# 1/rms by token from the row form by 32x32 turns on VectorE, in place of two-column matmuls, in a fused decoder layer on one core

## The chip, the cores and the metric

One core of a Trainium2 chip runs the whole program. Its engines take their instructions in order, each from its own queue, and wait for each other by semaphores: TensorE (PE in the profile; PEld is its weight load), VectorE (DVE), ScalarE (ACT), GpSimd (POOL) and SyncE (SP), which here only issues DMAs. The metric is the device time of one execution in microseconds (us), as the median of several runs. A profile is one further execution, recorded by the hardware; its times count from the first instruction.

## The reference, cut to what matters

One decoder layer over 512 tokens of 1024 features, with a fixed memory of 256 tokens. What bears on the change are two of its norms and what is computed from them:

```python
def rms_norm(x, g):
    xf = x.astype(jnp.float32)
    var = jnp.mean(xf * xf, axis=-1, keepdims=True)
    return (xf * lax.rsqrt(var + EPS) * g.astype(jnp.float32)).astype(x.dtype)
...
        h = rms_norm(x, norm_mix[l])
        proj = h @ w_in[l]
        q_a, k_a, v_a, u_b, gate_b, gate_c, g_a, g_b = jnp.split(proj, split_points, axis=-1)
...
        x = x + memory_cross_attention(rms_norm(x, norm_mem_q[l]), rms_norm(mem, norm_mem_kv[l]),
                                       w_mem_q[l], w_mem_kv[l], w_mem_o[l])
```

Stick-breaking attention (8 heads of 64) on q, k, v, a gated short convolution, two gated branch projections and an output projection follow the first line; keys and values of the memory come from `rms_norm(mem, ...)`. A SwiGLU feed-forward part and a final norm end the layer.

## The kernel before

All matrices are split in two parts, high and low, and a product is three matmuls (high x high, high x low, low x high), made by `mm3` at lines 176 to 178. Weights come by DMA as 128x1024 tiles `wr`; ScalarE casts the high part `wh` (L167), VectorE subtracts for the low part `wl` (L170).

The norm's factor 1/rms is not applied to the activations but to the products, so it is needed in two forms. *Along* the free axis, the same on all 128 partitions, it scales outputs that have tokens along the row (q, k, gates, the convolution; `r0b` for the mixer, 512 wide, and `rmb` for the memory, 256 wide). *By token*, one number for each partition, it scales outputs that have tokens on the partitions: the attention's values `v` (through `r0`) and the memory's values `vm` (through `rm`). `squares_mean` (L198) holds both. Given the sums of squares `acc`, split in `acch` and `accl`, `along` multiplies them by a 128x128 matrix of 1/1024 into `varb` (two matmuls, L218); `by_token` uses each 128-token piece as the stationary side against two columns of that matrix, into `var` (L209): eight matmuls with 128x2 outputs for 512 tokens, four for 256. `rstd_of` (L124) then makes 1/sqrt by Ln and Exp on ScalarE and one Newton step on VectorE, once for each form.

Round the first use of these factors the program runs as follows. TensorE makes the value products `v` of all tokens (L282), then `varb` and `var`, then the projections `pr`, column block by column block. `stacked` (L262) evicts the values: ScalarE scales the high part by `r0` (L268), VectorE makes the low part (L269), eight times each. `qk_part` (L312) scales a `pr` by `r0b` into q or k and splits it; the later half of q is also copied by DMA into `late_q` (`lq` in the profile, L321), with zeros in the other head's rows, so that the two heads of a pair are scored by one matmul of 256 or 512 columns.

`scores` (L394) multiplies keys by queries into the bank `z` and makes from it, with e^-|z| and ln, log(1 + e^z) in `e` (L417 to L420), masked by GpSimd (L376). `parts` (L429) splits `e` in `l` (ScalarE L390, VectorE L391). `weights` (L449) adds `negtri` times `l` into the same bank `z` (L454), which gives the log of the attention weights; ScalarE takes exp (L462). The steps go over four head pairs and four key blocks; between them TensorE makes further `pr` blocks from the list `fill`. Within the loop over the steps TensorE's order is that of the code (`manual_schedule`); before that loop, and for ScalarE, VectorE, GpSimd and SP throughout this stage, the framework's scheduler sets the order from its own estimates and priorities. The first call, `scores(*steps[0])`, stands ahead of the loop, so where its three matmuls stand among the `pr` is the scheduler's choice.

The memory's sums of squares are gathered along the attention's steps; at step `MEAN_AT` = 14 `rm` and `rmb` are made. `mem_scale` is a part of the later memory sublayer; `mem_v` uses `rm`. `eps_sq` (L1129) belongs to the feed-forward part's norm, and `cu` (L340) is the convolution's input, in two buffers of 128x514.

Of the kernel before, what the change touches and what calls it, by code (L numbers as in the profile page):

```python
# [8 lines left out]
F32 = mybir.dt.float32  # L9
# [4 lines left out]
P = 128  # L14
D = 1024
S = 512
KD = D // P
TT = S // P
# [20 lines left out]
MEAN_AT = 14  # L39
# [11 lines left out]
def hybrid_layer(ctx: ExitStack, tc: tile.TileContext, xT_d, memT_d, cols_d, wv_d, win_d,  # L51
                 wbr_d, wmix_d, wmq_d, wmk_d, wmv_d, wmo_d, wfi_d, wfo_d, wfp_d, gain_d, wga_d, out):
    nc = tc.nc

    cpool = ctx.enter_context(tc.tile_pool(name="cpool", bufs=1))
# [13 lines left out]
    def nm(s):  # L69
        count[0] += 1  # L70
        return f"{s}{count[0]}"

    def unit(s, cols=512):
        return upool.tile([P, cols], F32R, tag="u", name=nm(s), padded_shape=[P, 512])

    def tmp(s, cols=512):
        return tpool.tile([P, cols], F32, tag="t", name=nm(s), padded_shape=[P, 512])

    def f(ap):
        return ap.bitcast(F32)  # L80
# [105 lines left out]
    def split(src, s, scale=None, cols=512, new=unit):  # L186

        hi, lo = new(s + "h", cols), new(s + "l", cols)
        if scale is None:
            casts.append(nc.scalar.copy(hi, src))  # L190
            los.append(nc.vector.tensor_tensor(out=lo, in0=src, in1=f(hi), op=ALU.subtract))
        else:
            nc.scalar.activation(hi, src, AF.Copy, scale=scale)
            nc.vector.scalar_tensor_tensor(out=lo, in0=src, scalar=scale, in1=f(hi),
                                           op0=ALU.mult, op1=ALU.subtract)
        return hi, lo

    def squares_mean(acc, n):  # L198

        parts = unit("acch", n * P), unit("accl", n * P)  # L200
        nc.vector.tensor_copy(parts[0], acc)
        nc.vector.tensor_tensor(out=parts[1], in0=acc, in1=f(parts[0]), op=ALU.subtract)

        def by_token(s, tables=(), bank=otile):

            vp = bank("var")
            for t in range(n):
                for i in range(2):
                    nc.tensor.matmul(vp[:, 2 * t:2 * t + 2], parts[i][:, t * P:(t + 1) * P],  # L209
                                     mean_r[:, 0:2], start=i == 0, stop=i == 1)  # L210
            return rstd_of(vp[:, 0:2 * n].rearrange("p (t two) -> p t two", two=2)[:, :, 0], n, s,
                           tables)

        def along(s, tables=(), bank=otile, keep=None):

            vp = bank("varb")[:, :n * P]
            for i in range(2):
                nc.tensor.matmul(vp, mean_r, parts[i], start=i == 0, stop=i == 1)  # L218
            return rstd_of(vp, n * P, s, tables, keep=keep)

        return by_token, along


    xg, wv = [], []
    acc0 = tmp("acc")
    x_raw = [f(unit("xk")) for _ in range(KD)]
# [33 lines left out]
    mean0 = squares_mean(acc0, TT)  # L260

    def stacked(src, scale, odd):  # L262


        u = unit("v").rearrange("p (a s d) -> p a s d", s=2, d=HD)
        hi, lo = u[:, :, odd, :], u[:, :, 1 - odd, :]
        src = src.rearrange("p (a b d) -> p a b d", b=2, d=HD)[:, :, odd, :]
        nc.scalar.activation(hi, src, AF.Copy, scale=scale)  # L268
        nc.vector.scalar_tensor_tensor(out=lo, in0=src, scalar=scale, in1=f(hi), op0=ALU.mult,  # L269
                                       op1=ALU.subtract)  # L270
        return u
# [3 lines left out]
    for k in range(KD):  # L275

        terms = ((0, 0), (0, 1), (1, 0))
        for some in ((term,) for term in terms) if k == 0 else (terms,):
            for t in range(TT):
                sl = slice(t * P, (t + 1) * P)  # L280
                for a, b in some:
                    nc.tensor.matmul(vps[t], xg[k][a][:, sl], wv[k][b],  # L282
                                     start=k == 0 and (a, b) == (0, 0),
                                     stop=k == KD - 1 and a == 1)
    r0b, r0 = mean0[1]("r0b"), mean0[0]("r0")
    v = [[stacked(vps[t], r0[:, t:t + 1], h) for h in range(2)] for t in range(TT)]


# [36 lines left out]
    def gate(m, j):  # L325
        ps = project((O_A, O_B)[j] + m * P)
        t = gates[m, j] = tmp("g")
        both.append(nc.vector.tensor_tensor(out=t, in0=ps, in1=r0b, op=ALU.mult))
# [172 lines left out]
    def mem_square(k2):  # L501

        mk = f(unit("mk")).rearrange("p (j t) -> p j t", j=2)
        load_mem(k2, mk)
        nc.scalar.activation(accm if k2 == 0 else mk, mk, AF.Square)
        if k2 > 0:
            nc.vector.tensor_tensor(out=accm, in0=accm, in1=mk, op=ALU.add)
        if k2 == KD // 2 - 1:
            nc.vector.tensor_tensor(out=accm[:, 0, :], in0=accm[:, 0, :], in1=accm[:, 1, :],
                                    op=ALU.add)  # L510
# [19 lines left out]
    def fill_some(to):  # L530
        while fill and n_fill - len(fill) < to:
            g, *args = fill.pop(0)
            g(*args)
# [5 lines left out]
    with tc.manual_schedule(engines={mybir.EngineType.PE}):  # L539
        for i in range(len(steps) + 1):  # L540
            if i in MEM_AT:
                mem_square(MEM_AT.index(i))
            if i == MEAN_AT - 2:
                mean = squares_mean(accm[:, 0, :], MT)
            fill_some(n_fill * sum(shares[:i + 1]) / sum(shares))
            if i == MEAN_AT:
                with tc.high_priority(150):
                    rm = mean[0]("rm", bank=mmtile)
            if i + 1 < len(steps):
                scores(*steps[i + 1])  # L550
            if i < len(steps):
                weights(*steps[i])
            else:
                gate(EARLY, 0)
            if i + 1 < len(steps):
                parts(*steps[i + 1])
            if i > 0:
                values(*steps[i - 1])
            if i == MEAN_AT:
                with tc.high_priority(150):  # L560
                    rmb = mean[1]("rmb", bank=mmtile)
# [433 lines left out]
    def mem_scale():  # L995
        r1 = mean1[0]("r1", log_exp_tables(casts[-1]))
        nc.vector.tensor_scalar(out=r1s, in0=r1, scalar1=(D // MH) ** -0.5, scalar2=None,
                                op0=ALU.mult)

    km, vm, mq, scs, prs, pts = [], [[None] * 2 for _ in range(MT)], {}, {}, {}, {}  # L1000

    def mem_k(m):
# [14 lines left out]
    def mem_v(n):  # L1017
        pss = [mmtile("vm") for _ in range(MT)]
        for c in range(4):
            w = load_w(wmv_d[n, c], 512)  # L1020
            for j in range(2):
                k = 2 * c + j
                for t in range(MT):
                    sl = slice(t * P, (t + 1) * P)
                    mm3(pss[t], (mg[k][0][:, sl], mg[k][1][:, sl]),
                        (w[0][:, j, :], w[1][:, j, :]), k == 0, k == KD - 1)
        for t in range(MT):
            vm[t][n] = split(pss[t], "vm", rm[:, t:t + 1])

    def mem_q(h):  # L1030
        b = banks.pop(QM + h)
# [94 lines left out]

    rms, eps_sq = f(unit("rms")), cpool.tile([P, S], F32, tag="eps_sq", name="eps_sq")  # L1129
    eps_t4 = spool.tile([P, TT], F32, tag="epst", name="epst", bufs=1)  # L1130
    eps_d = cpool.tile([P, P], F32, tag="eps_d", name="eps_d")
    yt = {}
# [26 lines left out]
    with tc.manual_schedule(engines={mybir.EngineType.PE, mybir.EngineType.Activation,  # L1159
# [6 lines left out]
        for n, (m, i) in enumerate(uses):  # L1166
# [25 lines left out]
            if (m, i) == (1, 6):  # L1192
# [3 lines left out]
                for t in range(TT):  # L1196
                    rows = slice(t * P // TT, (t + 1) * P // TT)
# [162 lines left out]
    with tc.manual_schedule(engines={mybir.EngineType.PE, mybir.EngineType.Activation,  # L1360
# [28 lines left out]
        r = norm(t)  # L1389
# [78 lines left out]
```

## Time and profile before

| what | value |
|---|---|
| median of 3 runs | 846.53 us (846.05 to 846.75) |
| the profiled execution, its span | 847.03 us, 845.3 us |
| granted TensorE clock, mean | 0.997 |
| moved by DMA | 120.47 MB |

The span reaches from the first to the last instruction; the profiled execution's own time has 1.7 us around it. A row of a timeline gives the start in us from the span's start, the duration in us, the engine, the line, the operation, what it writes and reads, the shapes, and a count where equal neighbours are merged; a bracket at its end tells how long the engine had been idle and what it waited for. A duration of a matmul includes its way through the array: matmuls of 512 columns follow each other at about 0.23 us though each is shown with 0.39.

### The profile page before, as it was taken

How to read it: one execution, taken by the hardware profiler on the slowest of the kernel's cores; microseconds unless marked ns; L12 is line 12 of the kernel's file. 1: busy time of each engine (PE TensorE's matmuls, PEld its weight loads, DVE VectorE, ACT ScalarE, POOL GpSimd, SP SyncE). 2: the span in 40 equal slices, each digit the busy share in tenths (PEclk: the TensorE clock that was granted, in tenths of full speed). 3: DMA queues.
4: the chain of work that ended last, by engine and by line, in shares of the span. 5: the costliest groups of instructions: out<-in, count | busy, mean ns of one | idle time of the engine just before them, and what ended most of it. 6: DMA issues, size and time to landing. Idle time of an engine off the chain costs nothing.

```text
span 845.3 us, 13478 instructions
## 1 busy us (share of the span) xinstructions
PE 835.7 (99%) x5095; PEld 748.2 (89%) x5095; DVE 669.3 (79%) x1152; ACT 482.9 (57%) x873; POOL 88.5 (10%) x113
## 2 busy tenths in 40 slices
PE   9999999999999999999999999999999999999996
PEld 7888787888899988999988899999999999888885
DVE  8769889987856867978775889888877778895764
ACT  7556767566534555766554766555455556554434
POOL 1011112210100011000000111211111110110013
PEclk9999999999999999999999999999999999999998
DMA  8332332314745484555331437777777763870112
GB/s 299 128 122 64 108 104 66 111 51 167 206 104 146 148 251 128 162 178 194 129 115 56 112 86 202 189 185 177 179 182 178 180 156 125 269 216 26 51 50 100
DMA packets 50257, 120.47 MB, mean 143 GB/s; under 512 B 5136, under 2 KB 8208, under 8 KB 50192
## 3 DMA queue, kind: packets, MB, share of 16 engines
q1 hardware_dynamic: 40656, 101.49, 36.2%
q0 software_dynamic: 9248, 17.83, 13.0%
q8 instruction: 40, 0.66, 0.3%
q10 hardware_dynamic: 288, 0.29, 0.1%
q14 instruction: 25, 0.20, 0.1%
HBM read 116.42 MB, written 2.10 MB: 140 GB/s over the span
## 4 chain that ended last, share of the span: by engine, by line
PE 99%; DVE 0%; ACT 0%; issue 0%; DVEq 0%; ACTq 0%
PE z L775 20%; PE y L775 10%; PE pr L176 6%; PE pr L177 6%; PE pr L178 6%; PE v L775 5%; PE r L176 3%; PE r L178 3%; PE r L177 3%; PE f L177 3%; PE f L176 3%; PE f L178 3%; PE v L282 3%; PE br L177 2%; PE br L176 2%; PE br L178 2%
## 5 line engine op out<-in xcount | busy, mean ns | idle before, releaser
L167 ACT CAST wh<-wr 128x1024 fp32r<-128x1024 f32 x82 | 85.6, 1048 | 51.8 <-PE pr L177 11.3
L170 DVE TENSOR_TENSOR wl<-wr,wh 128x1024 fp32r<-128x1024 f32 x82 | 99.9, 1222 | 18.7 <-ACT wh L167 17.9
L775 PE MATMUL z<-xdh,wf 128*128 128x256 f32 x480 | 94.6, 282 | 0.0
L176 PE MATMUL pr<-xgh,wh 128*128 128x512 f32 x224 | 87.8, 392 | 0.0
L178 PE MATMUL pr<-xgh,wl 128*128 128x512 f32 x224 | 87.3, 390 | 0.0
L177 PE MATMUL pr<-xgl,wh 128*128 128x512 f32 x224 | 87.3, 390 | 0.0
L775 PEld LDWEIGHTS z<-xdh,wf 128*128 128x128 f32 x480 | 77.5, 189 | 0.3 <-issue 0.2
L775 PE MATMUL z<-xdl,wf 128*128 128x256 f32 x240 | 67.0, 279 | 0.0
L799 ACT COPY sa<-z 128x256 f32<-128x256 f32 x52 | 19.4, 373 | 74.1 <-PE z L775 74.0
L766 DVE TENSOR_TENSOR wf<-s,wf 128x512 fp32r<-128x512 f32 x60 | 41.4, 691 | 22.8 <-ACT wf L765 21.6
L725 POOL DMA_DIRECT2D ws<-in_w_ffn_in_dram x22 | 26.5, 1203 | 299.0 <-DVE c L619 109.5
L752 DVE TENSOR_TENSOR wf<-wg,wf 128x1024 fp32r<-128x1024 f32 x30 | 36.8, 1226 | 18.1 <-ACT wf L749 18.1
L178 PEld LDWEIGHTS pr<-xgh,wl 128*128 128x128 f32 x224 | 42.0, 188 | 8.9
L176 PEld LDWEIGHTS pr<-xgh,wh 128*128 128x128 f32 x224 | 42.1, 188 | 8.6 <-DVE rv L135 0.3
L177 PEld LDWEIGHTS pr<-xgl,wh 128*128 128x128 f32 x224 | 42.1, 188 | 8.3
L775 PE MATMUL y<-xch,wf 128*128 128x256 f32 x240 | 49.0, 286 | 0.0
L775 PE MATMUL z<-xch,wf 128*128 128x256 f32 x240 | 48.1, 283 | 0.0
L775 PEld LDWEIGHTS z<-xdl,wf 128*128 128x128 f32 x240 | 45.4, 189 | 0.2
L177 PE MATMUL f<-wl,acth 128*128 128x512 f32 (+1 forms) x116 | 44.3, 382 | 0.0
L176 PE MATMUL f<-wh,acth 128*128 128x512 f32 (+1 forms) x116 | 44.3, 382 | 0.0
L178 PE MATMUL f<-wh,actl 128*128 128x512 f32 (+1 forms) x116 | 44.1, 382 | 0.0
L766 DVE TENSOR_TENSOR wf<-ws,wf 128x512 fp32r<-128x512 f32 x60 | 40.9, 682 | 1.4 <-ACT wf L765 1.3
(357 smaller groups left out, 2466.3 us busy)
## 6 DMA issues: line engine op xcount, KB each, us to landing
wr<-in_w_in_dram SPq DMA_DIRECT2D x28, 512.0 KB, 3.5
ws<-in_w_ffn_in_dram SPq DMA_DIRECT2D x22, 512.0 KB, 3.8
ws<-in_w_ffn_in_dram POOLq DMA_DIRECT2D x22, 512.0 KB, 5.8
wg<-in_w_ffn_in_dram SPq DMA_DIRECT2D x22, 512.0 KB, 4.2
wr<-in_w_ffn_out_dram SPq DMA_DIRECT2D x14, 512.0 KB, 4.4
a<-in_w_ffn_in_dram SPq DMA_DIRECT2D x22, 256.0 KB, 4.4
wr<-in_w_branch_dram SPq DMA_DIRECT2D x8, 512.0 KB, 3.5
wr<-in_w_mix_out_dram SPq DMA_DIRECT2D x8, 512.0 KB, 3.7
```

Source lines behind the costliest of these rows:

```text
L167: after(nc.scalar.copy(h2, raw), lead[-1:] + waiting[:1])
L170: lows.append(nc.vector.tensor_tensor(out=l2, in0=raw, in1=f(h2), op=ALU.subtract))
L176: nc.tensor.matmul(ps, a[0], b[0], start=start, stop=False, **kw)
L177: nc.tensor.matmul(ps, a[0], b[1], start=False, stop=False, **kw)
L178: nc.tensor.matmul(ps, a[1], b[0], start=False, stop=stop, **kw)
L282: nc.tensor.matmul(vps[t], xg[k][a][:, sl], wv[k][b], start=k == 0 and (a, b) == (0, 0), stop=k == KD - 1 and a == 1)
L725: nc.gpsimd.dma_start(s13, a[:, 0:4:3, :], accum_op=ALU.add)
L752: nc.vector.tensor_tensor(out=lo, in0=pair, in1=f(hi), op=ALU.subtract)
L766: nc.vector.tensor_tensor(out=lo, in0=raw, in1=f(hi), op=ALU.subtract)
L775: nc.tensor.matmul(ps[:, :HS], a, b, start=i < 3 and k == 0 and j == 0, stop=k == KP - 1 and j == 2, skip_group_check=True)
L799: nc.scalar.copy((s[:, :HS], None, None, s[:, HS:], t[:, :HS], t[:, :HS])[i], z)
```

## The change

`by_token_of` is new. It takes the row form, where all 128 partitions hold the same numbers, and for each of the four groups of 32 partitions turns one 32x32 block of each 128-token piece on VectorE: group g takes the tokens 32g to 32g + 31 of every piece. After the turn, partition 32g + i holds the factor of token 32g + i of piece t in each of 32 columns, and column 0 is used. This gives `r0` from `r0b` (four instructions on 32 partitions x 128 elements) and `rm` from `rmb` (four of 32 x 64). The calls of `by_token` for the mixer and the memory go, with their narrow matmuls, Ln, Exp and Newton step; the query norm of the memory sublayer (`r1`) keeps its own. `rm` is written in `mem_scale` now. `eps_sq` takes a buffer of `cu` instead of one of its own.

```diff
+    def by_token_of(row, s):
+
+        n = row.shape[1] // P
+        r = cpool.tile([P, n, 32], F32, tag=s, name=nm(s))
+        for g in range(TT):
+            rows = slice(32 * g, 32 * g + 32)
+            nc.vector.transpose(out=r[rows, :, :],
+                                in_=row.rearrange("p (t c) -> p t c", c=P)[rows, :, rows])
+        return r[:, :, 0]
...
-    r0b, r0 = mean0[1]("r0b"), mean0[0]("r0")
+    r0b = mean0[1]("r0b")
+    r0 = by_token_of(r0b, "r0")
...
-            if i == MEAN_AT:
-                with tc.high_priority(150):
-                    rm = mean[0]("rm", bank=mmtile)
...
+        rm.append(by_token_of(rmb, "rm"))
+
+    rm = []
...
-            vm[t][n] = split(pss[t], "vm", rm[:, t:t + 1])
+            vm[t][n] = split(pss[t], "vm", rm[0][:, t:t + 1])
...
-    rms, eps_sq = f(unit("rms")), cpool.tile([P, S], F32, tag="eps_sq", name="eps_sq")
+    rms, eps_sq = f(unit("rms")), cpool.tile([P, S], F32, tag="cu", name="eps_sq",
+                                                 bufs=2, padded_shape=[P, S + 2])
```

How the queues read after it, at three places (the changed file has other line numbers, and its buffers other numbers). TensorE at the end of the value products, before:

```order
L218 MATMUL varb_332<-accl_229,mean_r 128x512
L209 MATMUL var_345<-mean_r,acch_228 128x2
L209 MATMUL var_345<-mean_r,accl_229 128x2
L209 MATMUL var_345<-mean_r,acch_228 128x2
L209 MATMUL var_345<-mean_r,accl_229 128x2
L209 MATMUL var_345<-mean_r,acch_228 128x2
L209 MATMUL var_345<-mean_r,accl_229 128x2
L209 MATMUL var_345<-mean_r,acch_228 128x2
L209 MATMUL var_345<-mean_r,accl_229 128x2
L176 MATMUL pr_407<-xgh_152,wh_403 128x512
```

and TensorE there after the change:

```order
L218 MATMUL varb_332<-acch_228,mean_r 128x512
L218 MATMUL varb_332<-accl_229,mean_r 128x512
L176 MATMUL pr_393<-xgh_152,wh_389 128x512
L177 MATMUL pr_393<-xgl_153,wh_389 128x512
L178 MATMUL pr_393<-xgh_152,wl_390 128x512
L176 MATMUL pr_393<-xgh_157,wh_389 128x512
```

The eight matmuls into `var` are gone, and `pr` follows `varb`.

TensorE at the first scores. Before, the last two of the three matmuls that write the scores of step 0 (bank `z_479`; `lq_388` and `lq_389` are the copied query's high and low parts, `qkh_475` and `qkl_476` the key's):

```order
L178 MATMUL pr_502<-xgh_197,wl_499 128x512
L176 MATMUL pr_502<-xgh_207,wh_498 128x512
L403 MATMUL z_479<-lq_389,qkh_475 128x256
L403 MATMUL z_479<-lq_388,qkl_476 128x256
L177 MATMUL pr_502<-xgl_208,wh_498 128x512
```

TensorE still before, 17 `pr` matmuls further on: the scores of step 1 (`z_556`), and behind them the `negtri` matmuls of step 0 with `l_490` and `l_491`:

```order
L177 MATMUL pr_543<-xgl_178,wh_539 128x512
L178 MATMUL pr_543<-xgh_177,wl_540 128x512
L403 MATMUL z_556<-lq_388,qkh_475 128x512
L403 MATMUL z_556<-lq_389,qkh_475 128x512
L403 MATMUL z_556<-lq_388,qkl_476 128x512
L454 MATMUL z_479<-l_490,negtri 128x256
L454 MATMUL z_479<-l_491,negtri 128x256
L176 MATMUL pr_543<-xgh_187,wh_539 128x512
```

After the change all of it fits in one stretch of TensorE's queue; the same bank is `z_465`, step 1's is `z_542`, and the parts are `l_476` and `l_477`:

```order
L414 MATMUL z_465<-lq_375,qkh_461 128x256
L414 MATMUL z_465<-lq_374,qkl_462 128x256
L178 MATMUL pr_529<-xgh_167,wl_526 128x512
L176 MATMUL pr_529<-xgh_177,wh_525 128x512
L177 MATMUL pr_529<-xgl_178,wh_525 128x512
L178 MATMUL pr_529<-xgh_177,wl_526 128x512
L414 MATMUL z_542<-lq_374,qkh_461 128x512
L414 MATMUL z_542<-lq_375,qkh_461 128x512
L414 MATMUL z_542<-lq_374,qkl_462 128x512
L465 MATMUL z_465<-l_476,negtri 128x256
L465 MATMUL z_465<-l_477,negtri 128x256
L176 MATMUL pr_529<-xgh_187,wh_525 128x512
```

The scores of step 0 stand 13 `pr` matmuls later (80 of them ahead of the last score matmul instead of 67), while step 1's scores and the `negtri` pair have kept their place behind the 84th `pr`: 4 `pr` matmuls lie between, where there were 17.

ScalarE at the same place. Before, from a weight cast and the key's cast to step 1's |z|:

```order
L167 CAST wh_685<-wr_683 128x1024
L190 CAST qkh_475<-qk_473 128x512
L417 ACTIVATE e_483<-z_479 128x256
L418 ACTIVATE e_483<-e_483 128x256
L419 ACTIVATE e_483<-e_483 128x256
L167 CAST wh_724<-wr_722 128x1024
L190 CAST qkh_529<-qk_527 128x512
L427 COPY carry_397<-z_479 1x256
L390 CAST l_490<-e_483 128x256
L417 ACTIVATE e_560<-z_556 128x512
```

and ScalarE there after the change:

```order
L167 CAST wh_710<-wr_708 128x1024
L428 ACTIVATE e_469<-z_465 128x256
L429 ACTIVATE e_469<-e_469 128x256
L190 CAST qkh_515<-qk_513 128x512
L430 ACTIVATE e_469<-e_469 128x256
L428 ACTIVATE e_546<-z_542 128x512
L429 ACTIVATE e_546<-e_546 128x512
L438 COPY carry_383<-z_465 1x256
L401 CAST l_476<-e_469 128x256
```

The weight cast that stood behind ln (`wh_724`, now `wh_710`) stands ahead of |z|, the cast of the next query (`qkh_515`) ahead of ln, and step 1's |z| and exp (`e_546`) ahead of the carry row and of the cast of `l` for step 0.

On SP, the two copies of the query's low half (`lq` from `qkl`) stand behind the next 512 KB weight load, where they stood ahead of it. On VectorE the four turns stand right behind the product that ends `r0b`, where the three narrow products stood among the wide ones; the turns of the memory's row stand among the last attention steps.

## The prediction

> **What bounds the kernel now.** I read the page's totals first, then the list of waits for TensorE alone, then the timeline round the places that the change touches.
>
> ```profile
> span 845.3 us, 13478 instructions
> PE 835.7 (99%) x5095; PEld 748.2 (89%) x5095; DVE 669.3 (79%) x1152; ACT 482.9 (57%) x873; POOL 88.5 (10%) x113
> PE 99%; DVE 0%; ACT 0%; issue 0%; DVEq 0%; ACTq 0%
> PE warm L241 <- DVE mean_f L104: 1.6, 1, 1.6
> ```
> Line two: TensorE is busy for 835.7 of 845.3 us. Line three, shares of the chain that ended last: TensorE 99%. Line four is the whole answer to "who did TensorE's matmuls wait for": 1.6 us once, before the first warm-up matmul. So TensorE never waits for data again. Whatever is taken from its queue shortens the run one for one, and any wait put into its queue lengthens it one for one. Work on the other engines counts only if TensorE comes to wait for it.
>
> **What is removed: twelve narrow matmuls.** The timeline of TensorE at the end of the value products, and at the step that computed the memory's narrow mean (start, duration, line, tiles):
>
> ```profile
> 28.60 0.16 PE L209 MATMUL var<-mean_r,acch 128*128 128x2 f32 x1
> ...
> 29.30 0.25 PE L209 MATMUL var<-mean_r,accl 128*128 128x2 f32 x1
> 29.41 0.48 PE L176 MATMUL pr<-xgh,wh 128*128 128x512 f32 x1
> 29.73 0.39 PE L177 MATMUL pr<-xgl,wh 128*128 128x512 f32 x1
> 29.96 0.40 PE L178 MATMUL pr<-xgh,wl 128*128 128x512 f32 x1
> ...
> 179.31 0.17 PE L209 MATMUL var<-mean_r,acch 128*128 128x2 f32 x1
> ...
> 179.74 0.49 PE L410 MATMUL z<-qkh,qkh 64*128 64x512 f32 x2
> ```
> The eight of the mixer's norm start at 28.60, where the first `pr` matmul would stand without them. The second `pr` starts at 29.73; one 512-column pitch (29.96 - 29.73 = 0.23) after 28.60 it would stand at 28.83. Saved: 0.90 us. The four of the memory's norm hold 179.31 to 179.74: saved 0.43 us. Together **-1.33 us**. The narrow Ln, Exp, Identity and products go from ScalarE and VectorE too, worth nothing by themselves since neither is waited for at those places.
>
> **What is added: VectorE's turns.** No 32x32 turn is in the trace, so its price is bounded by the nearest VectorE rows: the narrow product that it replaces, and a 32-partition sum of 256 elements per lane, twice a turn's 128.
>
> ```profile
> 32.46 0.15 DVE L142 SCALAR_TENSOR_TENSOR r<-ra,ry 128x4 f32<-128x4 f32 x1
> L441 DVE TENSOR_TENSOR e<-e,carry 32x256 f32<-32x256 f32 x12 | 4.9, 436 | 1.6 <-DMA carry<-carry 1.3
> ```
> Between 0.15 and 0.44 us each. I take the middle of the two, 0.29 (a turn has half the elements of the second row), so four cost 1.2 us; the three narrow products they replace cost about 0.5. (The Trainium skill, page "VectorE: DVE Perf Modes", section "The three transpose paths", gives 311 ns for a 128x128 bf16 turn on VectorE; by it four would be an estimated 1.2 us. No run here shows it yet.) The 1.2 us lie beside TensorE's `pr` matmuls, which need no r, so they cost nothing directly; they only make the value and query copies later. The four turns of the memory's row stand among VectorE's work at the end of the attention and feed `vm`, evicted from 423 us on: more than 200 us of cover, 0. `eps_sq` taking one of the conv's two `cu` buffers frees SBUF and waits for readers hundreds of us gone: 0.
>
> **What is moved: the first scores, and this costs more than the saving.** The list order in the change section shows it. Before, 17 `pr` matmuls stand between the last score matmul of `z_479` and those that write `negtri` times `l` into the same bank; now 4, with the three of the next scores behind them both times. Up to the `negtri` pair TensorE has the same 84 `pr` and 6 score matmuls in both kernels: the scores alone moved, 13 `pr` later. What has to happen between the two is in the trace of before:
>
> ```profile
> 44.98 0.28 PE L403 MATMUL z<-lq,qkl 128*128 128x256 f32 x1
> 45.10 0.39 PE L177 MATMUL pr<-xgl,wh 128*128 128x512 f32 x1
> 45.30 0.38 ACT L417 ACTIVATE e<-z 128x256 f32<-128x256 f32 x1 [3.33 <-PE z L403]
> 45.71 0.42 ACT L418 ACTIVATE e<-e 128x256 f32<-128x256 f32 x1
> 46.16 0.42 ACT L419 ACTIVATE e<-e 128x256 f32<-128x256 f32 x1
> 46.48 1.04 ACT L167 CAST wh<-wr 128x1024 fp32r<-128x1024 f32 x1
> 47.06 0.41 DVE L420 SCALAR_TENSOR_TENSOR e<-z,e 128x256 f32<-128x256 f32 x1
> 47.42 0.61 ACT L190 CAST qkh<-qk 128x512 fp32r<-128x512 f32 x1
> 47.55 0.41 POOL L376 TENSOR_SCALAR_AFFINE_SELECT e<-e 128x256 f32<-128x256 f32 x1 [42.88 <-DVE e L420]
> 47.94 0.36 ACT L427 COPY carry<-z 1x256 f32<-1x256 f32 x1
> 48.20 0.40 ACT L390 CAST l<-e 128x256 fp32r<-128x256 f32 x1
> 48.95 0.41 DVE L391 TENSOR_TENSOR l<-e,l 128x256 fp32r<-128x256 f32 x1
> 48.98 0.63 PE L403 MATMUL z<-lq,qkh 128*128 128x512 f32 x2
> 49.44 0.40 PE L403 MATMUL z<-lq,qkl 128*128 128x512 f32 x1
> 49.68 0.39 PE L454 MATMUL z<-l,negtri 128*128 128x256 f32 x2
> 49.88 0.60 ACT L417 ACTIVATE e<-z 128x512 f32<-128x512 f32 x1 [1.27 <-PE z L403]
> 49.91 0.40 PE L176 MATMUL pr<-xgh,wh 128*128 128x512 f32 x1
> 50.51 0.63 ACT L418 ACTIVATE e<-e 128x512 f32<-128x512 f32 x1
> 51.04 0.37 ACT L462 ACTIVATE a<-z 128x256 f32<-128x256 f32 x1
> ```
> Before: scores start at 44.98; ScalarE makes |z|, exp, ln; VectorE max and sum; GpSimd the mask; ScalarE the carry row and the high part of `l`; VectorE the low part, done at 48.95 + 0.41 = 49.36; TensorE comes for it at 49.68. Slack 0.3 us.
>
> Now, with the same durations. TensorE: the `pr` pitch is (48.98 - 45.10) / 17 = 0.228. The last score matmul starts at 44.98 - 0.90 + 13 x 0.228 = 47.04. TensorE reaches the `negtri` pair at 49.68 - 0.90 = 48.78, and could start the `pr` behind it at 49.91 - 0.90 = 49.01. ScalarE's queue after the change is |z|, exp, cast of `qkh`, ln, then |z| and exp of the *next* scores (128x512), carry row, cast of `l`. Steps from start to start in the rows above: 47.04 + 0.32 (45.30 - 44.98) = 47.36 for |z|; + 0.41 exp 47.77; + 0.32 (46.48 - 46.16, the next one not needing its result) the cast 48.09; + 0.52 (47.94 - 47.42) ln 48.61; the next |z| needs the last of the three next scores, 48.78 - 0.24 (49.68 - 49.44), and + 0.44 (49.88 - 49.44) is 48.98; + 0.63 exp 49.61; + 0.53 (51.04 - 50.51) the carry row 50.14. Meanwhile ln ends at 48.61 + 0.42 = 49.03; VectorE, which first makes the low part of the query cast, takes e at about 49.4, GpSimd 0.49 later (47.55 - 47.06), and the carry row can start 0.39 (47.94 - 47.55) behind that, at 50.24. Then + 0.26 (48.20 - 47.94) the cast of `l` 50.50, + 0.40 its end 50.90, VectorE + 0.41 and two hand-overs of 0.05 (a guess from the gaps here) 51.41. TensorE starts the second `negtri` matmul there, the next `pr` 0.12 (45.10 - 44.98) later at 51.53 instead of 49.01: **a wait of +2.5 us**, on an engine that had none.
>
> Its bounds: with nothing between the dependent steps (no cast, no next scores, no carry row ahead of `l`) the steps 0.32, 0.41, 0.45 (46.16 - 45.71), 0.47, 0.49, 0.39, 0.45, 0.46 and the last 0.12 end at 50.60, a wait of 1.6. If each of eight hand-overs is 0.1 slower, 3.3. I keep 2.5, the queue as it stands.
>
> **What feeds the scores.** The second score matmul needs the low half of q in `late_q`, copied by DMA. SP now issues a 512 KB weight load between the high and the low copies. The rows: the high copies of before, that order as it happens once in before, and the times to landing of its two:
>
> ```profile
> 40.56 1.18 SPq L321 DMA_DIRECT2D lq<-qkh  x2
> ...
> 118.24 0.54 SPq L158 DMA_DIRECT2D wr<-in_w_in_dram  x1
> 118.87 1.10 SPq L321 DMA_DIRECT2D lq<-qkl  x2
> ...
> wr<-in_w_in_dram SPq DMA_DIRECT2D x1, 512.0 KB, 4.2
> lq<-qkl SPq DMA_DIRECT2D x1, 64.0 KB, 3.7
> ```
> The copy behind a load lands 0.63 + 3.7 = 4.3 us after the load was issued. ScalarE now makes a weight cast (1.04 us above) ahead of the first query's cast instead of behind it, and the turns push the values ahead of that; I take the high copies 0.8 us later. Then the load goes out at 40.56 + 0.8 + 1.18 = 42.5 and the copy lands near 46.9, just when TensorE gets there (47.04 - 0.12). I add 0.1 and keep 0 to 0.7 as the range.
>
> **Sum.** -0.90 - 0.43 + 2.5 + 0.1 = **+1.3 us**. Made against the profiled execution: 847.03 us with its span of 845.3, so 848.3. That execution is 0.50 above the median of the runs shown, 846.53; against the median, 847.8. That is +0.15%; a difference under 0.2% (1.7 us: 844.8 to 848.2) is about what a measurement of this kernel can't tell from no change.
>
> **Rivals.**
> *The saving stands alone* (0.10). The hand-over to `l` is so much quicker than read that TensorE hardly waits: 845.2 to 846.0. For it: before has 0 wait at this spot. Against: that spot had 4.7 us (44.98 to 49.68) for the chain and now has 1.75; even the bare chain takes 3.4.
> *The low half of q comes late* (0.25), the case that ends slower. The scores' second matmul waits for the copy, and the whole chain behind it moves along one for one. It starts when the turns cost more than I took: at 0.44 each, up to +0.6 us on the value and query copies, with no slack left at 46.92 to absorb it; with the copy at the late end of its range +0.7 more. 1.3 + 0.6 + 0.7 is +2.6: 849.1. It decides the sign from +0.4 us on, a landing later than 47.3.
> *The array's clock falls back in the new gap* (0.04).
>
> ```profile
> 1.61 3.78 PE L241 MATMUL warm<-neg 128*128 128x512 f32 x8 [1.61 <-DVE mean_f L104]
> 5.29 2.05 PE L282 MATMUL v<-wvh,xgh 128*128 128x512 f32 x4
> 7.14 1.21 PE L282 MATMUL v<-wvl,xgh 128*128 128x512 f32 x4
> ```
> At the start 12 matmuls of 512 columns run at (7.14 - 1.61) / 12 = 0.46 us against 0.23 later: 2.8 us lost. If a wait of 2.5 us brought that back once more, 850.6. (The Trainium skill, page "TensorE: Matmul & The Clock Gate", section "Part 1: The HAM clock gate", has the array return to half clock after an idle window of about 3.4 us. By that rule the gap, shorter and broken by one matmul, leaves the clock alone and the sum stays; with the rule tripped it is the price above. The slow start agrees with half clock; no gap in before tests the rest.)
> *Something unread* (0.06), spread evenly.
>
> **How the numbers follow.** The forecast, a wait between 1.6 and 3.0 us, has 0.55: net +0.4 to +1.7, no measurable change except at its upper edge and with an unlucky median (0.47 same, 0.08 slower). The saving alone: 0.07 same, 0.03 faster, since even -1.33 is inside 0.2%. Late copy: 0.24 slower, 0.01 same. Clock: 0.04 slower. Unread: 0.02 each. Sum: faster 0.05, same 0.57, slower 0.38. The range, 845.8 to 849.6, leaves out most of the saving alone below and the clock above.
>
> **What would show it.** In the list of TensorE's waits after the change, the `negtri` pair of the first scores waiting 1.6 to 3.0 us in all, near 48.8 to 51.5, for ScalarE's and VectorE's `l`; `pr` right behind `varb` at 28.60; turns of 0.15 to 0.44 us; no wait for `rm`. I am wrong if TensorE shows no wait there, if the wait is at the score matmuls for `lq` instead, or if a second stage differs.

## The result, and the profile after

After: 849.3 us, median of 8 runs (847.96 to 851.84). Before, in runs beside them: 846.85 us, 8 runs (846.05 to 847.16). The ratio is 1.0034, 95% interval 1.0025 to 1.0043: 2.45 us slower. The time lies inside the forecast's range, 1.5 us above its 847.8; the forecast called it no measurable change, and it is a measurable loss. The spread is new too: 3.9 us, where before has 1.1. Three of the eight executions, 850.25 to 851.84, have a mean granted TensorE clock of 0.994 or 0.995. Before has 0.996 to 0.998 in the runs further below, apart from three disturbed executions of 1180 to 1681 us, which are left out of every number here.

The profiled execution of after took 848.9 us at clock 0.997. Two lines of its page:

```profile
span 847.1 us, 13446 instructions
PE 834.8 (99%) x5083; PEld 746.0 (88%) x5083; DVE 669.9 (79%) x1154; ACT 482.1 (57%) x867; POOL 86.5 (10%) x113
```

And the list of TensorE's waits (us in total, times, longest):

```profile
PE z L465 <- ACT l L401: 1.9, 1, 1.9
PE warm L251 <- DVE mean_f L104: 1.6, 1, 1.6
PE z L783 <- ACT sa L807: 0.4, 1, 0.4
PE z L414 <- DMA lq<-qkl: 0.3, 1, 0.3
```

TensorE's busy time fell by 0.9 us (835.7 to 834.8) and the span grew by 1.8, although this execution started quicker: its `varb` matmuls stand 0.77 us earlier (the second at 27.60, in before at 28.37). No changed instruction of TensorE lies ahead of them, and the same program has the second at 28.34 in a later profile (e9), so this belongs to the single execution; two traces are compared below from a common row, not by their times. Waits that before did not have stand there: 1.9 us at the `negtri` pair, 0.3 at a score matmul for the low half of q, 0.4 at 347 us. TensorE's timeline at these places (start, duration, line, tiles, in brackets the idle time ahead and what ended it):

```profile
27.60 0.39 PE L218 MATMUL varb<-accl,mean_r 128*128 128x512 f32 x1
27.83 0.40 PE L176 MATMUL pr<-xgh,wh 128*128 128x512 f32 x1
...
45.99 0.39 PE L177 MATMUL pr<-xgl,wh 128*128 128x512 f32 x1
46.66 0.36 PE L414 MATMUL z<-lq,qkh 128*128 128x256 f32 x1 [0.28 <-DMA lq<-qkl]
46.85 0.28 PE L414 MATMUL z<-lq,qkl 128*128 128x256 f32 x1
46.98 0.39 PE L178 MATMUL pr<-xgh,wl 128*128 128x512 f32 x1
...
48.36 0.40 PE L414 MATMUL z<-lq,qkl 128*128 128x512 f32 x1
50.66 0.84 PE L465 MATMUL z<-l,negtri 128*128 128x256 f32 x2 [1.90 <-ACT l L401]
51.35 0.39 PE L176 MATMUL pr<-xgh,wh 128*128 128x512 f32 x1
```

Three readings. `pr` stands right behind `varb`, at 27.83: the narrow matmuls are gone. From the `pr` at 45.99 to the next at 46.98, with two score matmuls between, are 0.99 us; without a wait a `pr` pitch and two short score matmuls take 0.23 + 2 x 0.12 = 0.47 (0.12 is 45.10 - 44.98 in before), so the late low half costs 0.5, more than the 0.28 in brackets. (The same stretch costs 0.3 to 0.4 in the profiles of e2, e5 and e9, which list no wait there.) From the last score matmul to the `pr` behind the `negtri` pair are 51.35 - 48.36 = 2.99 us; before 49.91 - 49.44 = 0.47: the new wait is 2.5 us in all, 1.9 ahead of the pair's first matmul and the rest ahead of its second, which is folded into its row. What TensorE waited for, on ScalarE, GpSimd and VectorE:

```profile
47.92 0.60 ACT L190 CAST qkh<-qk 128x512 fp32r<-128x512 f32 x1
48.42 0.41 ACT L430 ACTIVATE e<-e 128x256 f32<-128x256 f32 x1
48.80 0.60 ACT L428 ACTIVATE e<-z 128x512 f32<-128x512 f32 x1
49.42 0.63 ACT L429 ACTIVATE e<-e 128x512 f32<-128x512 f32 x1
49.65 0.41 POOL L387 TENSOR_SCALAR_AFFINE_SELECT e<-e 128x256 f32<-128x256 f32 x1 [44.97 <-DVE e L431]
49.96 0.34 ACT L438 COPY carry<-z 1x256 f32<-1x256 f32 x1
50.21 0.40 ACT L401 CAST l<-e 128x256 fp32r<-128x256 f32 x1
50.64 0.42 DVE L402 TENSOR_TENSOR l<-e,l 128x256 fp32r<-128x256 f32 x1 [1.06 <-ACT l L401]
```

The order is the one that the prediction wrote down: query cast, ln, the next scores' |z| and exp, the mask, the carry row, then the two parts of `l`. The turns, in the list of groups by line (busy time in all, mean ns of one):

```profile
L230 DVE STREAM_TRANSPOSE r<-r0b 32x128 f32<-32x128 f32 x4 | 1.2, 302 | 0.1
L230 DVE STREAM_TRANSPOSE rm<-rmb 32x64 f32<-32x64 f32 x4 | 0.9, 234 | 0.1
```

And SyncE's queue at the copies of q, where the weight load stands between the high and the low ones:

```profile
40.73 1.18 SPq L332 DMA_DIRECT2D lq<-qkh  x2
42.00 0.54 SPq L158 DMA_DIRECT2D wr<-in_w_in_dram  x1
42.62 1.10 SPq L332 DMA_DIRECT2D lq<-qkl  x2
```

### The profile page after: what moved, and what is told of

The parts are those of the page before. It is cut to its first block, busy times and chain, and to the rows that moved or that the text cites. A ratio compares the mean times of both kernels' runs of the same rounds, so it can differ in the third digit from the quotient of the medians.

```text
span 847.1 us, 13446 instructions
## 1 busy us (share of the span) xinstructions
PE 834.8 (99%) x5083; PEld 746.0 (88%) x5083; DVE 669.9 (79%) x1154; ACT 482.1 (57%) x867; POOL 86.5 (10%) x113
## 4 chain that ended last, share of the span: by engine, by line
PE 95%; DVE 2%; ACT 1%; DMA 1%; issue 1%; SPq 0%; ACTq 0%; DVEq 0%
PE z L783 20%; PE y L783 10%; PE pr L176 6%; PE pr L177 6%; PE pr L178 6%; PE v L783 5%; PE f L178 3%; PE f L177 3%; PE f L176 3%; PE r L178 3%; PE r L176 3%; PE r L177 3%; PE v L292 3%; PE br L176 2%; PE br L178 2%; PE br L177 2%
```

## The experiments

Three theories. **W**: TensorE's wait at the first scores is the loss, and the order that the scheduler chose makes it. **C**: besides, in some executions the array's clock drops after that wait. **T**, the rival: the turns themselves cost time. All ran in five rounds beside before. "Over 850" counts executions above 850 us; all of these have a clock of 0.994 to 0.996, and in no kernel of the table without them did an execution pass 849.35.

| kernel | median us (runs) | before beside it | ratio, 95% | over 850 |
|---|---|---|---|---|
| after (as first timed) | 849.3 (8) | 846.85 | 1.0034, 1.0025 to 1.0043 | 3 of 8 |
| e1 memory's part alone | 846.51 (11) | 846.58 | 0.9997, 0.9988 to 1.0006 | 0 |
| e2 mixer's part alone | 849.54 (5) | 846.58 | 1.0039, 1.0027 to 1.0051 | 2 of 5 |
| e3 after, 12 matmuls moved | 851.1 (6) | 846.58 | 1.0047, 1.0034 to 1.0059 | 5 of 6 |
| e4 before, 12 matmuls moved | 848.99 (5) | 846.58 | 1.0031, 1.0018 to 1.0043 | 1 of 5 |
| e5 after, gap filled | 848.26 (11) | 846.56 | 1.0019, 1.0011 to 1.0028 | 0 |
| e6 before, scores late (80) | 848.3 (11) | 846.56 | 1.002, 1.0011 to 1.0029 | 0 |
| e7 after, half units | 846.46 (11) | 846.56 | 0.9998, 0.9989 to 1.0007 | 0 |
| e8 before, half units | 847.69 (11) | 846.56 | 1.0013, 1.0004 to 1.0021 | 0 |
| e9 after again | 850.42 (6) | 846.74 | 1.0035, 1.0023 to 1.0046 | 4 of 6 |
| e10 after, low q on GpSimd's queue | 848.32 (11) | 846.74 | 1.002, 1.0011 to 1.0029 | 0 |
| e11 e10 and a half unit | 846.42 (11) | 846.74 | 0.9999, 0.999 to 1.0008 | 0 |
| e12 before, scores later (83) | 850.15 (5) | 846.74 | 1.0032, 1.0019 to 1.0045 | 3 of 5 |
| e13 after, low q first | 846.76 (11) | 846.56 | 1.0004, 0.9995 to 1.0012 | 0 |
| e14 e13 and a half unit | 845.55 (11) | 846.56 | 0.9991, 0.9982 to 1.0 | 0 |

### Which part: e1 and e2

```diff
 e1 (against after)
-    r0 = by_token_of(r0b, "r0")
+    r0 = mean0[0]("r0")
 e2 (against after)
+            if i == MEAN_AT:
+                with tc.high_priority(150):
+                    rm_narrow = mean[0]("rm", bank=mmtile)
...
-        rm.append(by_token_of(rmb, "rm"))
+        rm.append(rm_narrow)
```

> The memory's norm alone is taken by turns; the mixer's norm has its eight narrow matmuls again, and TensorE's order at the first scores is that of before. Theory W (the lost time is TensorE's wait at the first scores, which the mixer's half of the change brings): no wait there, so only the four narrow matmuls go: 0.43 us below before, ratio about 0.9995, granted clock 0.997 as before. Rival T (turns on VectorE cost time wherever they stand, or the extra 0.7 us at 347 us comes from rm): 0.3 us or more above before.

> The mixer's norm alone is taken by turns; the memory's has its four narrow matmuls again. TensorE's order at the first scores is that of after. Theory W: the whole loss is here: after plus 0.43 us, so about 2.9 us above before (ratio 1.0034), with a wait of 1.9 us or more at the negtri pair in the profile. Theory C (in about half of the executions the array's clock drops after that wait, besides): the same, with a mean granted clock of 0.994 to 0.996 in some executions and a spread of 3 us or more. Rival T: 0.5 us or less above before.

The memory's part alone is 0.07 us below before in the medians, 0.3 by the ratio; its interval, 1.0 us below to 0.5 above, holds both the expected 0.43 and nothing. The mixer's part alone has the whole loss (849.54, the same 1.9 us wait) and the spread. The loss comes with the mixer's part.

### Covering the wait, first try: e3 and e4

A piece of 12 projection matmuls moved from the fourth step's share to the first's, in after and, as a control, in before.

```diff
-FILL = ((3, 3, 3, 3), (2, 2, 3, 4))
+FILL = ((4, 3, 3, 2), (2, 2, 3, 4))
```

> After, with one of the 12-matmul pieces of projection that stand between the scores taken from the fourth step of the first pair and put in the first, ahead of the first negtri pair (4,3,3,2 in place of 3,3,3,3); the work is the same. Theory W: the chain on ScalarE and VectorE gets 12 x 0.227 = 2.7 us more cover, the wait of 1.9 us at the first negtri pair goes: 1.9 to 2.5 us below after, that is 0.3 to 0.8 us below before (ratio to before 0.9990 to 0.9997), unless the fourth step then waits. Theory C: the granted clock is 0.997 in every execution and the spread falls to about 1 us, median 846.0 to 846.5. Rival T: as after, 849.3.

> Before, with the same piece of projection moved from the fourth step to the first: the control for the run above. Before has no wait at the first negtri pair to cover, so theory W expects the time of before within 0.3 us (ratio 1.000). If it is faster than before by as much as the run above is faster than after, the piece's place is worth something of its own and the run above says nothing of the wait.

Both expectations missed: after lost 1.8 us more and before lost 2.4. The "unless" of e3 is what came. The first `negtri` pair no longer waits, but the fourth step's four matmuls do. e3's list of TensorE's waits:

```profile
PE z L465 <- DVE l L402: 1.4, 2, 0.7
PE z L465 <- ACT l L401: 0.6, 1, 0.6
```

And its windows there (us from the span's start, length, busy time and count of PE, PEld, DVE, ACT and POOL, then the granted clock, DMA share, GB/s):

```profile
78.00:80.00 2.00, 0.81 (x2) 0.40 (x3) 1.94 (x5) 2.00 (x4) 0.00 (x0) 1.00 0.00 0
80.00:82.00 2.00, 1.30 (x4) 0.90 (x4) 2.00 (x4) 1.61 (x4) 0.31 (x1) 0.64 0.00 0
82.00:84.00 2.00, 2.00 (x7) 1.81 (x7) 2.00 (x4) 1.13 (x3) 1.03 (x2) 0.50 0.16 41
84.00:86.00 2.00, 2.00 (x6) 1.55 (x5) 1.93 (x5) 0.55 (x2) 0.34 (x1) 0.50 0.76 213
86.00:94.00 8.00, 8.00 (x34) 6.53 (x33) 3.36 (x6) 3.47 (x6) 0.00 (x0) 0.91 0.14 43
```

The waits sum to 2.0 us in three pieces, and here the clock's fall is seen: 1.00, then 0.64, 0.50, 0.50, 0.91. e4 waits at the same matmuls, also 2.0 us in three pieces (0.5, 0.8 and 0.7), but its clock stays at 1.00 there in the profile, and one of its five executions passed 850 us. So the move says nothing for or against W, since it opened another wait as large; but it caught what C needs.

### Is it the clock, and what sets it: e5, e9, e6 and e12

e5 fills after's gap with eight matmuls of constants; nothing reads their bank. e9 is after itself. e6 and e12 have no turn: they are before, with the first step's score matmuls put where after has them (e6), and the two late ones three places later still (e12).

```diff
 e5 (against after), behind the second step's scores
+            if i == 0:
+                idle = otile("idle")
+                for _ in range(8):
+                    nc.tensor.matmul(idle, neg1, neg1[:, None, :].broadcast_to([P, S // P, P]),
+                                     start=True, stop=True)
 e6 (against before): scores emitted at a count of projection matmuls; e12: 83 for 80
-    scores(*steps[0])
-    parts(*steps[0])
+    at[69] = lambda: scores(*steps[0], 0)
+    at[80] = lambda: (scores(*steps[0], 1), parts(*steps[0]))
```

> After, with eight 512-column matmuls of constants (8 x 0.227 = 1.8 us, into a bank that nothing reads) between the second step's score matmuls and the first negtri pair, where TensorE waits 1.9 us: the wait stays as long as it is, but the array is busy in it. Theory C (in some executions the array's clock falls to half for some microseconds because of the gap, as the run with the unit moved shows in its windows): no execution with a granted clock below 0.996, spread near 1 us, median at after's undisturbed time, 848.0 to 849.0. Theory W alone (the wait is all; the spread is noise): the spread of after stays, 3 us or more, and the median is 849.3 or a little above, since eight matmuls were added.

> After itself, unchanged, beside the runs below on the same chip: more executions for the spread. Theory C: the executions fall in two groups, near 848.3 at clock 0.997 or 0.998 and at 850 to 852 at 0.994 to 0.996, with a quarter to three quarters of them in the second. Theory W alone: one group about 849.3. The extra 0.7 us at 347 us in the profile of after: absent from this profile if it was that execution's late load, there again if it belongs to the order of after.

> Before, every narrow matmul kept, with the first step's score matmuls put where after has them: the first behind 69 projection matmuls of 512 columns and not 62, the other two behind 80 and not 67, so that 4 and not 17 stand before the second step's scores. No turn is in it. Theory W: TensorE waits 2.0 to 2.8 us at the first negtri pair, 848.9 to 849.6 where the clock holds; with theory C some executions at 851 to 852.5 and clock 0.994 to 0.996. Rival T (the turns or their place on VectorE make the wait): no wait, 846.8.

> Before, every narrow matmul kept and no turn, with the first step's two late score matmuls behind 83 projection matmuls and not 80, so that one and not four stand before the second step's scores: a gap 3 x 0.227 = 0.7 us longer than in the run with 80, which waited 1.4 us and kept its clock in 11 executions. Theory C (the length of the gap decides): a wait of about 2.1 us, some executions (a quarter or more) at 851 to 853 and clock 0.994 to 0.996, the rest near 849.0. Theory W alone: all near 849.0, spread about 1 us.

e9's executions fall in two groups, as C said: 848.1 and 848.46 at clock 0.997, and 850.32 to 851.09 at 0.994 and 0.995. Its profile was taken in one of the second, and shows the fall. Windows, as above:

```profile
50.00:52.00 2.00, 0.68 (x2) 0.48 (x3) 0.81 (x3) 1.72 (x4) 0.41 (x1) 0.92 0.40 105
52.00:54.00 2.00, 2.00 (x6) 1.61 (x6) 0.92 (x3) 0.85 (x2) 0.81 (x2) 0.50 0.18 45
54.00:56.00 2.00, 2.00 (x7) 1.56 (x7) 0.56 (x2) 0.00 (x0) 0.00 (x0) 0.72 0.01 1
```

And TensorE's timeline:

```profile
51.25 1.04 PE L465 MATMUL z<-l,negtri 128*128 128x256 f32 x2 [1.91 <-ACT l L401]
52.09 0.63 PE L176 MATMUL pr<-xgh,wh 128*128 128x512 f32 x1
52.52 0.63 PE L177 MATMUL pr<-xgl,wh 128*128 128x512 f32 x1
...
55.08 0.42 PE L177 MATMUL pr<-xgl,wh 128*128 128x512 f32 x1
55.33 0.40 PE L178 MATMUL pr<-xgh,wl 128*128 128x512 f32 x1
```

The wait is the same as in the first profile of after, 1.91 us. But behind it the `pr` matmuls come every 0.43 us (52.52 - 52.09) and not every 0.23, until 55.08. The windows give what it cost: 2 x (1 - 0.92) + 2 x (1 - 0.50) + 2 x (1 - 0.72) = 1.7 us. With the gap filled (e5), the wait is off the list and the clock stays in e5's windows:

```profile
50.00:52.00 2.00, 1.85 (x9) 1.20 (x8) 1.43 (x3) 1.24 (x4) 0.36 (x1) 1.00 0.44 107
52.00:54.00 2.00, 2.00 (x10) 1.66 (x9) 0.74 (x3) 0.70 (x3) 0.45 (x2) 1.00 0.02 5
```

More work in the same place, and the kernel is faster: 848.26, none of 11 over 850, spread 1.8 us. That is after without the fall: 1.7 us above before. (After's own seven executions below 850 us have a median of 848.75.)

e6 shows that the order is enough: without a turn, before waits 1.4 us and loses 1.7. This is 0.6 to 1.3 less than I expected, since ScalarE there casts `l` ahead of the next scores' exp (49.73 and 50.31 in its trace; in after 50.21 and 49.42). With three matmuls fewer between (e12), the wait is 2.1 us, and the fall is there, again without a turn; its executions with a fall took 850.15 to 850.64, less than the 851 to 853 that I expected. The rows of the wait in e6's list and in e12's:

```profile
PE z L466 <- ACT carry L439: 1.4, 1, 1.4
```
```profile
PE z L466 <- ACT carry L439: 2.1, 1, 2.1
```

Of e12 the windows behind the wait:

```profile
52.00:54.00 2.00, 2.00 (x8) 1.51 (x7) 1.48 (x3) 0.96 (x2) 0.77 (x2) 0.62 0.06 12
54.00:56.00 2.00, 2.00 (x6) 1.58 (x5) 0.42 (x1) 0.00 (x0) 0.00 (x0) 0.53 0.00 0
```

A wait of 1.4 us: none of 11 executions falls. One of 1.9: seven of 14 (after and e9) and two of five (e2). One of 2.1: three of five. These counts go by the time, over 850 us; the trace shows the fall itself in the profiles of e3, e9 and e12. So T falls and both W and C stand. One rival is left for the two kernels that kept their clock: e5 and e6 ran on one chip, without a run of after beside them. On the chip of e9 and e12, where the falls came, e10 and e11 with a wait of 1.0 us had none in 22 executions, so there it goes by the wait; that in e5 the fill and in e6 the shorter wait kept the clock, and not their chip, is therefore argued and not shown.

### What gives the saving back: e7, e8, e10, e11, e13, e14

e7 and e8 take the cover in halves of six matmuls from the two steps that have slack; e10 and e11 take the first head pair's low copies of q off SyncE's queue; e13 and e14 keep them there but hold the weight load back until the first of them is issued.

```diff
 e7, e8 (projections opened in quarters, go_on does the next quarter)
-FILL = ((3, 3, 3, 3), (2, 2, 3, 4))
+FILL = ((8, 5, 5, 6), (4, 4, 6, 8))
...
-        fill.extend([(open_project, col), (g, *args)])
+        fill.extend([(open_project, col), (go_on,), (go_on,), (g, *args)])
 e10 (against after); e11 has it and FILL (7, 6, 5, 6)
-                nc.sync.dma_start(f(t)[hs, h, :], f(u)[hs, HS:])
+                (nc.gpsimd if t is late_q[0][1] and p == 0 else nc.sync).dma_start(f(t)[hs, h, :], f(u)[hs, HS:])
 e13 (against after), in load_raw; e14 has it and FILL (7, 6, 5, 6)
+        loads.append(i)
+        if len(loads) in (10,):
+            after(i, low_q[2:3])
...
-                nc.sync.dma_start(f(t)[hs, h, :], f(u)[hs, HS:])
+                low_q.append(nc.sync.dma_start(f(t)[hs, h, :], f(u)[hs, HS:]))
```

> After, with 12 projection matmuls more ahead of the first negtri pair, taken in halves of 6 from the second and the third step, where the profile of before leaves 2.3 and 2.9 us between the chain's end and its negtri matmuls (0.8 in the fourth, from which the run before took them): steps of 48, 30, 30 and 36 in place of 36 each. Theories W and C: no wait at any negtri matmul above 0.3 us, clock 0.997 throughout, spread about 1 us; after minus 1.9 to 2.5 (wait) minus the executions at the lower clock: 845.7 to 846.6, 0.2 to 1.0 us below before. Rival T: as after.

> Before with the same two halves moved (48, 30, 30, 36): the control for the run above. Theory W: before's time within 0.3 us, no wait at a negtri matmul; then the run above minus this one is what the narrow matmuls alone are worth, 0.9 to 1.3 us.

e7 takes the loss away but wins nothing, where I expected 0.2 to 1.0 us; e8 says why: with the halves moved, before itself loses 1.1 us, against my 0.3. New waits stand on e8's list, 0.5 us at the memory's narrow mean and 0.3 at a `negtri` matmul. e7 minus e8, the change at equal places of the projection matmuls, is 846.46 - 847.69 = -1.23 us, near the forecast's 1.33. Part of that agreement may be chance: e8's 0.5 us stand at a matmul that the change removes, and e7 alone loses 0.3 us at the low half of q.

> After, with the two copies of the low half of q for the first step issued on GpSimd's queue and not behind the 512 KB weight load on SyncE's; the scheduler then puts the two late score matmuls 4 projection matmuls earlier (76 and not 80 ahead of them, 8 and not 4 behind). Theory W with its low-q term: no wait at these score matmuls (0.3 us and 0.2 to 0.5 us in weight loads go), the wait at negtri falls by 4 x 0.227 = 0.9 us to 1.0 to 1.4 us; too short a gap for the clock to fall: 847.0 to 847.6, clock 0.997, spread near 1 us. Rival: copies on GpSimd's queue land no sooner, and nothing changes (849.3, with the spread).

> After, with the low half of q on GpSimd's queue as in the run above, and 6 projection matmuls of the third step put ahead of the first negtri pair (42, 36, 30, 36). Theories W and C: 6 x 0.227 = 1.4 us more cover takes the wait that is left to 0.3 us or less, the third step has 2.9 us to give and opens no wait; only the saved narrow matmuls stay: 1.0 to 1.3 us below before, 845.2 to 845.8, ratio 0.9985 to 0.9990, clock 0.997. If it stays at 846.4 as with the halves moved alone, what was lost there is not the low half of q.

e10 missed. The copies are issued at 43.42 on GpSimd's queue, 15.1 us behind the second `varb` matmul (28.35), where after issues them 15.0 behind it (42.62 - 27.60): no sooner. They take a median 3.2 us to land, no less than SyncE's 3.2, and the scores, now earlier, wait 1.0 us for them where they had waited 0.3:

```profile
PE z L414 <- DMA lq<-qkl: 1.0, 1, 1.0
PE z L465 <- ACT l L401: 0.2, 1, 0.2
```

e11 missed too: the wait at `negtri` is gone, the 1.0 us for q remains, and with it the kernel stays level with before (846.42).

> After, with the two copies of the low half of q issued ahead of the 512 KB weight load on SyncE's queue, as in before; the scheduler then puts the two late score matmuls behind 75 projection matmuls, with 9 and not 4 behind them. Theory W with its low-q term: no wait for the low half of q, and the wait at negtri falls by 5 x 0.227 us plus the 0.5 us of the low half to 0.8 to 1.4 us; the clock holds: 846.2 to 847.2, spread near 1.5 us. If the low half still waits 0.5 us or more, the order on the queue is not what makes it late.

> The same, with 6 projection matmuls of the third step put ahead of the first negtri pair (42, 36, 30, 36): both waits covered. Theory W: only the saved narrow matmuls stay, 1.0 to 1.3 us below before: 845.3 to 845.8, ratio 0.9984 to 0.9988, clock 0.997, spread near 1.5 us. If it stays within 0.4 us of before, as the versions with one of the covers did, something else than the two waits gives the saving back.

With the low copies ahead of the load on the same queue, issued 14.5 us behind the second `varb` matmul (42.20 - 27.70 in e13), the wait for them is gone. e13 keeps the rest of the `negtri` wait, 0.3 us on its list, and comes out level with before. e14 covers that as well. Its list of TensorE's waits:

```profile
PE warm L256 <- DVE mean_f L104: 1.6, 1, 1.6
```

SyncE's queue, and then TensorE's timeline:

```profile
42.16 1.10 SPq L339 DMA_DIRECT2D lq<-qkl  x2
43.31 3.78 SPq L160 DMA_DIRECT2D wr<-in_w_in_dram  x2
```
```profile
45.14 0.28 PE L421 MATMUL z<-lq,qkh 128*128 128x256 f32 x1
45.26 0.28 PE L421 MATMUL z<-lq,qkl 128*128 128x256 f32 x1
...
49.50 0.40 PE L472 MATMUL z<-l,negtri 128*128 128x256 f32 x2
49.74 0.40 PE L181 MATMUL pr<-xgh,wh 128*128 128x512 f32 x1
```

No wait is left but the first warm-up's. 845.55 us: 1.0 us below before in the medians, 0.8 by the ratio, at the edge of what can be told (upper end 1.0), and 3.7 below after as first timed. With the change in it and the order repaired, it clearly beats after; that it beats before too is likely, not shown.

## Why the prediction was wrong

- **What bounds the kernel**: right. Every wait put into TensorE's queue came out in the time.
- **What is removed, -1.33**: right, a little too large. Counted from the second `varb` matmul, the second `pr` moved from 1.36 us (29.73 - 28.37) to 0.46 (28.06 - 27.60): 0.90. Across the step of the memory's mean, from the last `pr` ahead of it to the first behind it, 3.08 us (182.16 - 179.08) became 2.73 (183.22 - 180.49): 0.35 and not 0.43. Together -1.25.
- **The turns, 0.29 us each, nothing on the path**: right. 0.302 and 0.234 us; four of the first kind took 1.25 us from first start to last end, and TensorE did not wait for them.
- **The moved scores, +2.5 at the `negtri` pair**: right, place, order and size (2.99 - 0.47 = 2.5).
- **The low half of q, +0.1**: mis-sized. 0.5 us in after's profile, 0.3 to 0.4 in those of e2, e5 and e9. The landing had no slack to begin with: TensorE came for it at 46.22 (one pitch of 0.23 after 45.99) and the copy let the matmul start at 46.66. The upper end of the term's range, 0.7, held it. e13 and e14 show that the order on the queue was the cause: with the low copies ahead of the load, the scores' second matmul comes 5 `pr` matmuls earlier and still loses nothing (in e14 45.14 and 45.26, 0.12 apart).
- **The sum of these**: -1.25 + 2.5 + 0.3 to 0.5 = +1.6 to +1.8. After with its gap filled (e5) measured 848.26 - 846.56 = +1.7. Without the clock, the forecast's +1.3 would have been 0.4 too low, mostly by the low half.
- **The limit of 0.2%, 1.7 us, below which nothing could be told: this step failed, and with it the call "no measurable change".** The intervals in the table reach about 0.1% to either side. The forecast's own +1.3 us, 0.15%, would have stood clear of that, and e5, which has no fall, does: 1.0011 to 1.0028. A loss was to be forecast from the sum as it stood.
- **The step that failed in the size is the rival "the array's clock falls back in the new gap", put at 0.04.** The prediction took its mechanism in, priced it at 2.8 us, and set it aside because the gap of 2.5 us was shorter than the window of about 3.4 us that it cited. It happens in seven of 14 executions of after and costs 1.7 us there; the group medians are 848.75 and 850.58. It is what lifts the median from 848.3 (e5) to 849.3 or, where more executions fell (e9), to 850.4. The price was too high, the chance far too low. That 849.3 lies inside the range is luck: the range's upper edge, 849.6, was there for a late copy of q and left the clock out, and e9, the same program, lies above it.

The rule that was leaned on is in the Trainium skill, page "TensorE: Matmul & The Clock Gate", section "Part 1: The HAM clock gate": half clock after an idle window of about 3.4 us, full clock after as long a busy one, with a window that runs freely, so that executions differ. Executions of one program do differ here, and the slow stretch at half clock, worked out from the windows above, is 2 x (0.08 + 0.50 + 0.28) / 0.5 = 3.4 us in e9, 2 x (0.38 + 0.47) / 0.5 = 3.4 us in e12 and (2 x (0.36 + 0.50 + 0.50) + 8 x 0.09) / 0.5 = 6.9 us in e3, once and twice that window: these parts agree. The idle window does not agree: in e9 and e12 the clock fell with no more than about 2.3 us without a matmul (in e12 the last score matmul starts at 48.92, a pitch of 0.23 before the gap, and the `negtri` pair at 51.47). In e12 the matmuls had then run at full pace for about 0.9 us before they slowed at 52.36. That would follow if a window of some 3.4 us is judged as a whole and a low share of work in it is enough, so that the phase of the window decides; no run here shows the window itself, and this stays a reading.

One thing stays open. After's profile has 0.7 us more at 347 us. A 512 KB weight load issued at 329.69 landed 4.3 us later, where in before it took 3.4 us (from the issue to the cast that waits for it), and the matmuls of the memory's queries came to wait. e9, the same program, does not have it, so it belongs to single executions; e2, e10 and e13 show it too. What makes that load late wasn't tried.

## What to carry to other kernels

When a few instructions are cut from the queue of the engine that bounds a kernel, compare the scheduled orders before pricing the cut: here 1.25 us were saved and about 3 us lost, because the scheduler moved the first scores next to what waits for them, and a 512 KB load ahead of two small copies. Where a new gap appears on TensorE, count the clock as a cost of its own (here 1.9 us of wait were enough in half of the executions, and 1.4 us in none), and look at more than one execution: a few with a lower granted clock and a wider spread are its mark. Fill the gap with useful matmuls if another step has the slack to give them, in pieces no larger than that slack.

## What the runs showed of the hardware

- The granted clock fell to 0.50 after gaps with 1.9 to 2.1 us of wait, in about half of the executions (12 of 24 of after, e9, e2 and e12, counted by a time over 850 us; seen in the traces of e9 and e12), and not in 11 executions with 1.4 us (e6). Three short waits close together, 2.0 us within 3.5 us, did it in five of six executions of e3 and in one of five of e4.
- Eight matmuls of constants in the gap kept the clock: 0 of 11 executions fell, and the kernel with more work was about 1 us faster than after.
- The copies of 64 KB issued on GpSimd's queue took 3.2 us to land, no less than the median of those on SyncE's queue in the same trace (3.2).
- The clock's fall lasted about 3.4 us at half rate in the traces of e9 and e12 and twice that in e3's, and so cost 1.7 us or more each time.
- The 32x32 turns of fp32 on 32 partitions took 302 ns at 128 elements a lane and 234 ns at 64.
